# The second MLP product of a decoder layer with the tokens stationary and 512 weight columns moving

## The chip, the core and the metric

The kernel runs on one core of a Trainium2 chip. The core has a matrix engine (TensorE; PE in the profile, and PEld for its weight loads), a vector engine (VectorE, DVE), a scalar engine (ScalarE, ACT), GpSimd (POOL, hardly used here) and a sync engine (SyncE, SP) that issues nearly all memory transfers (DMA). A matmul holds one operand, of up to 128 columns, still in TensorE's array (stationary, brought in by a weight load) and streams the columns of the other through it (moving); the result goes to PSUM, whose banks hold 512 fp32 values per partition. The other engines work in SBUF, which has 128 partitions. The metric is the device time of one execution in microseconds (us); here and below "median" is that of the repeated runs.

## The reference

One hybrid decoder layer and a final norm, in float32, for 256 tokens of width 2048. The part that matters here is the MLP and the last norm:

```python
h2 = _modulate(_rms_norm(x, norm2_g[l]), shift2, scale2)
ff = jnp.square(jax.nn.relu(jnp.einsum("bsd,df->bsf", h2, w_ff1[l])))
x = x + gate2[:, None, :] * jnp.einsum("bsf,fd->bsd", ff, w_ff2[l])
return _rms_norm(x, final_g)
```

`w_ff1` is 2048 x 8192, `w_ff2` 8192 x 2048. The six vectors shift1 to gate2 come from `silu(c) @ w_ada + b_ada`. Ahead of this stand a norm, a wide input projection, a linear recurrence, sliding-window attention and an output projection, which are the same in both kernels.

## The kernel before, in words

The activations lie with the channels on the partitions: a tile `x1[f]` holds 128 channels of the 256 tokens (sixteen of them). Weights are stationary, 128 x 128 at a time, and 256 tokens move. To keep float32 accuracy at a cheaper product, each operand is split into a rounded part and the exact rest (`float32r`), and each product is made of three passes: rounded x rounded, rounded x rest, rest x rounded (lines L176, L177, L178, in `gemm`).

From the projection on, the work is a stream of *units*. A unit is 1 MB of weights, 128 partitions x 2048 columns: it is loaded into one of four `raw` (rw) buffers (L152), split in two halves of 1024 columns, the rounded part by ScalarE (L160, wh) and the rest by VectorE (L162, wl), into three buffers each, and multiplied on TensorE, 48 matmuls of 256 columns. Weights are taken in two units ahead. Side work of the other engines is spread over the units from a list (`later`), and so is the making of the conditioning vector (`ada_unit`, 1 MB of `w_ada` and one VectorE reduction at L241). A scheduler sets the final order of each engine's queue from the data dependencies and the buffers; an engine then works its queue in order.

The MLP runs in four quarters `c`. A quarter makes 16 tiles of the hidden layer (`ff1_unit`, matmuls L656 to L658; evicted by L660 to L664 and split by L141, L142 into `ff[c, f]`), and then adds their share of the second product into all 16 tiles of x1 (`ff2_unit`). A second-product unit makes one output tile: its weights are stationary, the 16 hidden tiles move, and VectorE evicts with the gate and the sum in one operation:

```python
ps = gemm(w, 0, [ff[c, j] for j in range(16)])
ve.scalar_tensor_tensor(out=x1[f], in0=ps, scalar=mod[:, 5 * KT + f:5 * KT + f + 1], in1=x1[f],
                        op0=ALU.mult, op1=ALU.add)
```

In the first quarter each such unit first forces the conditioning unit of its own gate (`flush(5 * KT + f + 1)`). In the last quarter ScalarE squares each finished tile and VectorE sums the squares (L134, L135); ScalarE then multiplies the tile with the norm's g (L684).

At the end the squares are summed over the partitions by matmuls with a column of ones (L754), and the 16 tiles are turned to token rows by 32 transposes on TensorE (L747), because 1/rms is then a scalar per partition: `rstd_cols` (L104 to L110) makes it, VectorE and ScalarE scale eight tiles of 128 tokens x 512 channels out of PSUM (L762, L764), and SP stores them (L765).

## Time and profile before

| | |
|---|---|
| median of 3 runs | 1605.51 us (1603.79 to 1606.83) |
| span of the profiled execution | 1604.2 us |
| granted TensorE clock, mean | 0.992 |
| TensorE, matmuls | 1567.8 us busy, 98% |
| VectorE / ScalarE | 73% / 53% busy |
| memory traffic | 388.27 MB, mean 242 GB/s |

The profile is of one execution, whose own time is its span, 1604.2 us, from the first to the last instruction; it is 1.3 us under the median. In rows of instructions stand the start, the length (both us), the engine, the line, the operation, the output and inputs with their shapes, and in brackets the idle time ahead of it with what ended it. Groups give the count, the mean length in ns, and the idle time before. In the tables by stage stand, after the stretch and its length, busy time and count of PE, PEld, DVE, ACT and POOL, then the granted clock as a share, the DMA engines' share, and GB/s. Matmuls are pipelined: one that is listed with 0.28 us can start 0.12 us after the one ahead. The pitch from start to start is what counts.

### The profile page before, as it was taken

The page shows a single profiled execution, that of the slowest core. Times are in us where ns is not written, and L with a number is a line of the kernel's source. Part 1 is how long each engine was busy: PE and PEld are TensorE (multiplying, and loading weights), DVE is VectorE, ACT ScalarE, POOL GpSimd, SP SyncE. Part 2 cuts the span into 40 slices and gives each one's busy share as a digit, 9 for nine tenths or more (in the row PEclk, how much of TensorE's full clock was granted, in tenths as well). Part 3 has the DMA queues.
Part 4 walks back from the last instruction along what each step waited for, and adds up shares of the span by engine and source line. Part 5 has one row for each costly group of instructions (what it writes and reads, how often), then busy time and mean ns, then how long its engine had stood idle before and what let it go on. Part 6 is the DMA issues. An engine that isn't in the chain of part 4 may idle for free.

```text
span 1604.2 us, 30912 instructions
## 1 busy us (share of the span) xinstructions
PE 1567.8 (98%) x12924; PEld 1542.5 (96%) x12924; DVE 1168.7 (73%) x1830; ACT 849.0 (53%) x1345; POOL 0.2 (0%) x4
## 2 busy tenths in 40 slices
PE   5999999999999999999999999999999999999998
PEld 4999998899999999999999999999999999999998
DVE  7798998898989678688787666865555555555554
ACT  5733447786886463344455553355434553355554
POOL 0000000000000000000000000000000000000000
PEclk7999999999999999999999999999999999999999
DMA  8898976557777777777976666865555555555552
GB/s 323 337 341 317 339 263 213 196 190 232 288 257 264 283 261 292 276 286 278 335 290 242 237 237 245 345 224 184 184 184 185 184 184 185 184 184 184 184 184 79
DMA packets 61724, 388.27 MB, mean 242 GB/s; under 512 B 6576, under 2 KB 11024, under 8 KB 19216
## 3 DMA queue, kind: packets, MB, share of 16 engines
q1 hardware_dynamic: 57168, 381.95, 65.6%
q10 hardware_dynamic: 4416, 4.35, 0.9%
q8 instruction: 101, 1.65, 0.4%
q14 instruction: 39, 0.32, 0.1%
HBM read 384.13 MB, written 2.15 MB: 241 GB/s over the span
## 4 chain that ended last, share of the span: by engine, by line
PE 86%; DVE 6%; DMA 3%; ACT 2%; issue 2%; SPq 0%; ACTq 0%; DVEq 0%
PE pg L178 20%; PE pg L176 20%; PE pg L177 20%; PE pg L656 8%; PE pg L657 8%; PE pg L658 8%; DMA ra<-in_wada_dram 2%; DVE wl L162 2%; PE pg L186 1%; DVE ra L241 1%; ACT wh L160 1%; PE pa L470 1%; PE pa L477 1%; DVE k L536 1%; DMA rw<-in_w_p_dram 0%
## 5 line engine op out<-in xcount | busy, mean ns | idle before, releaser
L160 ACT ACTIVATE wh<-rw 128x1024 fp32r<-128x1024 f32 (+2 forms) x534 | 545.5, 1023 | 656.4 <-PE pg L177 446.9
L176 PE MATMUL pg<-k,wh 128*128 128x256 f32 x3072 | 867.3, 283 | 11.0 <-ACT k L141 9.0
L178 PE MATMUL pg<-k,wl 128*128 128x256 f32 x3072 | 862.9, 282 | 3.5 <-DVE wl L162 3.3
L177 PE MATMUL pg<-k,wh 128*128 128x256 f32 x3072 | 865.0, 282 | 0.3 <-DVE k L142 0.2
L162 DVE TENSOR_TENSOR wl<-rw,wh 128x1024 fp32r<-128x1024 f32 (+2 forms) x534 | 628.4, 1178 | 286.7 <-ACT wh L160 285.0
L176 PEld LDWEIGHTS pg<-k,wh 128*128 128x128 f32 x3072 | 580.1, 189 | 13.8 <-ACT k L141 9.5
L178 PEld LDWEIGHTS pg<-k,wl 128*128 128x128 f32 x3072 | 580.3, 189 | 6.2 <-DVE wl L162 4.9
L177 PEld LDWEIGHTS pg<-k,wh 128*128 128x128 f32 x3072 | 580.2, 189 | 1.6 <-DVE k L142 0.9
L656 PE MATMUL pg<-z,wh 128*128 128x258 f32 x1024 | 289.8, 283 | 0.0
L657 PE MATMUL pg<-z,wh 128*128 128x256 f32 x1024 | 289.1, 282 | 0.0
L658 PE MATMUL pg<-z,wl 128*128 128x258 f32 x1024 | 288.5, 282 | 0.0
L241 DVE CUSTOM_DVE_ANT_0 ra<-ra,scr,vc 128x2048 f32<-128x2048 f32 x96 | 225.0, 2346 | 16.0 <-DMA ra<-in_wada_dram 15.9
L658 PEld LDWEIGHTS pg<-z,wl 128*128 128x128 f32 x1024 | 194.9, 190 | 0.0
L657 PEld LDWEIGHTS pg<-z,wh 128*128 128x128 f32 x1024 | 194.4, 190 | 0.0
L656 PEld LDWEIGHTS pg<-z,wh 128*128 128x128 f32 x1024 | 193.7, 189 | 0.0
L673 DVE SCALAR_TENSOR_TENSOR k<-pg,mod,k 128x256 f32<-128x256 f32 x64 | 30.9, 483 | 38.9 <-PE pg L178 38.9
L660 DVE TENSOR_REDUCE sh<-pg 128x1 f32<-128x2 f32 x64 | 10.2, 159 | 37.6 <-PE pg L658 37.6
L663 ACT ACTIVATE t<-t,sh 128x256 f32<-128x256 f32 x64 | 31.7, 496 | 1.4 <-DVE t L662 1.4
L142 DVE TENSOR_TENSOR k<-t,k 128x256 fp32r<-128x256 f32 x64 | 27.2, 425 | 4.7
L314 DVE TENSOR_TENSOR k<-pg,k 128x256 f32<-128x256 f32 x64 | 25.8, 418 | 6.6 <-PE pg L178 4.0
L141 ACT ACTIVATE k<-k 128x256 fp32r<-128x256 f32 x64 | 24.3, 411 | 9.7 <-DVE k L602 5.6
L186 PE MATMUL pg<-k,rw 128*128 128x256 f32 x128 | 28.3, 379 | 0.0
(146 smaller groups left out, 755.5 us busy)
## 6 DMA issues: line engine op xcount, KB each, us to landing
rw<-in_w_f_dram SPq DMA_DIRECT2D x204, 1024.0 KB, 4.8
ra<-in_wada_dram SPq DMA_DIRECT2D x96, 1024.0 KB, 6.2
rw<-in_w_p_dram SPq DMA_DIRECT2D x31, 1024.0 KB, 5.7
rw<-in_w_r_dram SPq DMA_DIRECT2D x20, 768.0 KB, 4.6
rw<-in_w_r_dram SPq DMA_DIRECT2D x16, 640.0 KB, 4.3
bt<-ud ACTq DMA_DIRECT2D x8, 512.0 KB, 4.5
xt<-in_xt_dram SPq DMA_DIRECT2D x8, 256.0 KB, 5.4
lw<-in_lruw_dram SPq DMA_DIRECT2D x4, 512.0 KB, 6.3
```

Source lines behind the costliest of these rows:

```text
L160: se.activation(wh[:, :c], raw[:, o:o + c], AF.Copy)
L162: ve.tensor_tensor(out=wl[:, :c], in0=raw[:, o:o + c], in1=wh[:, :c].bitcast(F32), op=ALU.subtract)
L176: te.matmul(ps, lhsT=wh[:, w], rhs=hl[:, 0], start=k == 0, stop=False)
L177: te.matmul(ps, lhsT=wh[:, w], rhs=hl[:, 1], start=False, stop=False)
L178: te.matmul(ps, lhsT=wl[:, w], rhs=hl[:, 0], start=False, stop=k == n - 1)
L186: te.matmul(ps, lhsT=raw[:, e:e + P], rhs=xs[k // 2][:, k % 2], start=k == k0, stop=k == k1 - 1)
L241: r = ve.tensor_tensor_reduce(out=raw, in0=raw, in1=scr, scale=1.0, scalar=vc[:, V_BADA + c:V_BADA + c + 1], op0=ALU.mult, op1=ALU.add, ac ...
L656: te.matmul(ps, lhsT=wh[:, e], rhs=z[k][:, 0:258], start=k == 0, stop=False)
L657: te.matmul(ps[:, 0:256], lhsT=wh[:, e], rhs=z[k][:, 258:514], start=False, stop=False)
L658: te.matmul(ps, lhsT=wl[:, e], rhs=z[k][:, 0:258], start=False, stop=k == KT - 1)
L663: se.activation(t[:, 0], t[:, 0], AF.Relu, bias=sh)
L673: ve.scalar_tensor_tensor(out=x1[f], in0=ps, scalar=mod[:, 5 * KT + f:5 * KT + f + 1], in1=x1[f], op0=ALU.mult, op1=ALU.add)
```

## The change

The second product is turned round. The hidden layer's tokens become stationary (128 hidden channels x 128 tokens) and 512 weight columns move, so the output has tokens on the partitions and 512 channels in a full PSUM bank. A unit is still 1 MB, but now the weights of four output tiles x four hidden tiles; they are read from the same array in memory as four runs of 512 columns per partition. Its two halves of 1024 weights each hold two hidden tiles for all 512 output columns, and a matmul moves four runs of 128 columns. Four units `u` finish one block `q` of 512 output channels for the two token blocks `b`, which lie in two PSUM banks. The sums over the quarters stand in eight tiles `acc`: copied there by ScalarE in the first quarter, added by VectorE after. x1 is turned to token rows (`turn_x1`, tiles `xk`) beside the first quarter. Since gate2 and the last norm's g now run along the free dimension, they are made as lines that are the same on every partition, by a product of ones with a diagonal (`gate2_line`, `line_of`), beside the last quarter; there the gate, the residual sum, the square with its sum, and g are applied to each block. At the end only 1/rms remains, and eight scalings and stores.

The diff, without comments that were removed and without the loop that tells the two kinds of loads apart:

```diff
+    def w_load_rows(src):
+        raw = wp.tile([P, 4, 512], F32, tag="raw", name=nm("rw"), bufs=RAW_BUFS)
+        nc.sync.dma_start(out=raw, in_=src)
+        parts = []
+        for o in (0, 256):
+            wh = wp.tile([P, 4, 256], F32R, tag="wh", name=nm("wh"), bufs=WH_BUFS)
+            se.activation(wh, raw[:, :, o:o + 256], AF.Copy)
+            wl = wp.tile([P, 4, 256], F32R, tag="wl", name=nm("wl"), bufs=WH_BUFS)
+            ve.tensor_tensor(out=wl, in0=raw[:, :, o:o + 256], in1=wh.bitcast(F32), op=ALU.subtract)
+            parts.append((wh, wl))
+        return parts
...
+    def add_rows(run, q, u):
+        f0 = full[0] + 4 * q
+        units.append((run, w_f[f0:f0 + 4, :, u * 512:u * 512 + 512].rearrange("f p n -> p f n"), 2048, None))
+        if q == 3 and u == 3:
+            full[0] += 16
...
-    def ff2_unit(c, f):
+    xk, acc, g2b, gfb, cur2 = {}, {}, {}, {}, {}
+    ssf = sp.tile([P, 2, 4], F32, tag="ssf", name="ssf", bufs=1)
+
+    def turn_x1(q):
+        for b in range(2):
+            pt = bank([P, 512])
+            for i in range(4):
+                te.transpose(pt[:, i * P:(i + 1) * P], x1[4 * q + i][:, b * P:(b + 1) * P], idt)
+            xk[b, q] = kp.tile([P, 512], F32, tag="k2", name=nm("xk"))
+            se.activation(xk[b, q], pt, AF.Copy)
+
+    def gate2_line(q):
+        g2b[q] = line_of(mod[:, 5 * KT + 4 * q:5 * KT + 4 * q + 4])
+        gfb[q] = line_of(vc[:, V_GF + 4 * q:V_GF + 4 * q + 4])
+
+    def line_of(cols):
+        pc = bank([P, 512])
+        dg = tmp([P, 512])
+        ve.tensor_tensor(out=dg.rearrange("p (k f) -> p k f", k=4), in0=idt[:, None, :].broadcast_to((P, 4, P)),
+                         in1=cols[:, :, None].broadcast_to((P, 4, P)), op=ALU.mult)
+        te.matmul(pc, lhsT=ones, rhs=dg, start=True, stop=True)
+        o = kp.tile([P, 512], F32, tag="k2", name=nm("ln"))
+        se.activation(o, pc, AF.Copy)
+        return o
+
+    def ff2_unit(c, q, u):
         def run(w):
+            if c == 3 and u == 0:
+                if q == 0:
+                    flush(6 * KT)
+                later(1.0, gate2_line, q)
+            if u == 0:
+                for b in range(2):
+                    cur2[b] = pg.tile([P, 512], F32, tag="pg", name=nm("pg"))
+            for k in range(4):
+                wh, wl = w[k // 2]
+                e = slice(k % 2 * P, k % 2 * P + P)
+                hl = ff[c, 4 * u + k]
+                first, last = u == 0 and k == 0, u == 3 and k == 3
+                for b in range(2):
+                    t = slice(b * P, b * P + P)
+                    te.matmul(cur2[b], lhsT=hl[:, 0, t], rhs=wh[:, :, e], start=first, stop=False)
+                    te.matmul(cur2[b], lhsT=hl[:, 0, t], rhs=wl[:, :, e], start=False, stop=False)
+                    te.matmul(cur2[b], lhsT=hl[:, 1, t], rhs=wh[:, :, e], start=False, stop=last)
+            if u < 3:
+                return
+            for b in range(2):
+                if c == 0:
+                    acc[b, q] = kp.tile([P, 512], F32, tag="k2", name=nm("ac"))
+                    se.activation(acc[b, q], cur2[b], AF.Copy)
+                else:
+                    ve.tensor_tensor(out=acc[b, q], in0=cur2[b], in1=acc[b, q], op=ALU.add)
+                if c == 3:
+                    o, x_ = acc[b, q], xk[b, q]
+                    ve.tensor_tensor(out=o, in0=o, in1=g2b[q], op=ALU.mult)
+                    ve.tensor_tensor(out=o, in0=o, in1=x_, op=ALU.add)
+                    se.activation(x_, o, AF.Square, accum_out=ssf[:, b, q:q + 1])
+                    ve.tensor_tensor(out=o, in0=o, in1=gfb[q], op=ALU.mult)
             if c == 0:
-                flush(5 * KT + f + 1)
-            ps = gemm(w, 0, [ff[c, j] for j in range(16)])
...
-        add_unit(run)
+                later(1.0, turn_x1, q)
+        add_rows(run, q, u)
...
-    def turn(n):
...
-    rs3 = rstd_cols(pq)
+    ss3 = sp.tile([P, 2], F32, tag="ss1", name="ss3", bufs=1)
+    ve.tensor_reduce(out=ss3, in_=ssf, axis=mybir.AxisListType.X, op=ALU.add)
+    rs3 = rstd_cols(ss3)
     for n in range(8):
         q, b = divmod(n, 2)
-        pt = turned[n] if n < 2 else turn(n)
...
+        o = acc[b, q]
+        if n % 2:
+            se.activation(o, o, AF.Copy, scale=rs3[:, b:b + 1])
+        else:
+            ve.tensor_scalar(out=o, in0=o, scalar1=rs3[:, b:b + 1], scalar2=None, op0=ALU.mult)
         nc.sync.dma_start(out=out[b, :, q * 512:(q + 1) * 512], in_=o)
```

Up to the first second-product matmul the queues of all engines hold the same instructions in the same order. Three places differ in what the prediction speaks of. In the changed kernel the three passes of the second product are L733, L734 and L735, the transposes of x1 L697, the lines' diagonals and products L709 and L711, the sum over the quarters L743, the gate L746, the residual L747, the square L748, g L749, and the last sum, scalings and stores L815, L821 and L823, L824.

TensorE, the start of the second product in the first quarter, before (k is a hidden tile, pg the PSUM tile of the output):

```order
L177 MATMUL pg_11382<-k_10334,wh_11238 128x256
L178 MATMUL pg_11382<-k_10334,wl_11240 128x256
L176 MATMUL pg_11382<-k_10405,wh_11238 128x256
L177 MATMUL pg_11382<-k_10405,wh_11238 128x256
L178 MATMUL pg_11382<-k_10405,wl_11240 128x256
```

and in the changed kernel:

```order
L734 MATMUL pg_11383<-wl_11241,k_10335 128x512
L735 MATMUL pg_11383<-wh_11239,k_10335 128x512
L733 MATMUL pg_11384<-wh_11239,k_10335 128x512
L734 MATMUL pg_11384<-wl_11241,k_10335 128x512
L735 MATMUL pg_11384<-wh_11239,k_10335 128x512
L733 MATMUL pg_11383<-wh_11239,k_10406 128x512
```

One hidden tile now serves two groups of three matmuls, one for each block of tokens, and each matmul is twice as wide.

VectorE, between the first and the second product of the last quarter, before (wl is a rest part of weights; the first row is the last eviction of the first product):

```order
L662 TENSOR_TENSOR t_17542<-pg_17491,rs_10267 128x256
L162 TENSOR_TENSOR wl_17485<-rw_17481,wh_17483 128x1024
L142 TENSOR_TENSOR k_17546<-t_17542,k_17546 128x256
L162 TENSOR_TENSOR wl_17489<-rw_17481,wh_17487 128x1024
L673 SCALAR_TENSOR_TENSOR k_9190<-pg_17559,mod,k_9190 128x256
```

and in the changed kernel (L709's outputs t are the diagonals; the second product's splits are L178):

```order
L682 TENSOR_TENSOR t_16407<-pg_16356,rs_10268 128x256
L709 TENSOR_TENSOR t_16451<-idt,mod 128x512
L178 TENSOR_TENSOR wl_16350<-rw_16346,wh_16348 128x1024
L142 TENSOR_TENSOR k_16411<-t_16407,k_16411 128x256
L709 TENSOR_TENSOR t_16457<-idt,vc 128x512
L709 TENSOR_TENSOR t_16611<-idt,mod 128x512
L178 TENSOR_TENSOR wl_16354<-rw_16346,wh_16352 128x1024
L709 TENSOR_TENSOR t_16617<-idt,vc 128x512
L709 TENSOR_TENSOR t_16771<-idt,mod 128x512
L709 TENSOR_TENSOR t_16777<-idt,vc 128x512
L178 TENSOR_TENSOR wl_16418<-rw_16414,wh_16416 128x1024
L709 TENSOR_TENSOR t_16931<-idt,mod 128x512
```

All eight diagonals stand here, among the splits of the second product's first units; before, only the splits and the first eviction stood there. TensorE's two products with them follow the first unit of each block.

VectorE, the end of the program, before (from the last eviction on):

```order
L673 SCALAR_TENSOR_TENSOR k_10173<-pg_18498,mod,k_10173 128x256
L104 TENSOR_SCALAR st_18566<-pa_18561 128x2
L106 RECIPROCAL st_18566<-st_18566 128x2
L108 SCALAR_TENSOR_TENSOR st_18566<-st_18566 128x2
L109 TENSOR_TENSOR st_18566<-st_18566 128x2
```

and in the changed kernel:

```order
L743 TENSOR_TENSOR ac_11994<-pg_16904,ac_11994 128x512
L743 TENSOR_TENSOR ac_11996<-pg_16905,ac_11996 128x512
L746 TENSOR_TENSOR ac_11994<-ac_11994,ln_16934 128x512
L746 TENSOR_TENSOR ac_11996<-ac_11996,ln_16934 128x512
L747 TENSOR_TENSOR ac_11994<-ac_11994,xk_12003 128x512
L747 TENSOR_TENSOR ac_11996<-ac_11996,xk_12010 128x512
L749 TENSOR_TENSOR ac_11994<-ac_11994,ln_16940 128x512
L749 TENSOR_TENSOR ac_11996<-ac_11996,ln_16940 128x512
L815 TENSOR_REDUCE ss_17034<-ssf 128x2
L104 TENSOR_SCALAR st_17036<-ss_17034 128x2
```

Nine operations now stand between the last product and the first step to 1/rms, where one stood (its square and the matmuls with ones, on the other engines, stood there too).

More of the change, by code (lines that the diff above doesn't have):

```diff
@@ L666, in ff1_unit @@
         add_unit(run)
-    def ff2_unit(c, f):
-        def run(w):
-            if c == 0:
-                flush(5 * KT + f + 1)
-            ps = gemm(w, 0, [ff[c, j] for j in range(16)])
-            ve.scalar_tensor_tensor(out=x1[f], in0=ps, scalar=mod[:, 5 * KT + f:5 * KT + f + 1], in1=x1[f],
-                                    op0=ALU.mult, op1=ALU.add)
-            if c == 3:
-                if f == 0:
-                    stat[3] = sp.tile([P, T], F32, tag="asq", name=nm("asq"), bufs=1)
-                if f < 15:
-                    sumsq(stat[3], x1[f], f == 0)
-                else:
-                    stat[4] = tmp([P, T])
-                    se.activation(stat[4], x1[f], AF.Square)
-                se.activation(x1[f], x1[f], AF.Copy, scale=vc[:, V_GF + f:V_GF + f + 1])
-        add_unit(run)
+    xk, acc, g2b, gfb, cur2 = {}, {}, {}, {}, {}
@@ L713, in hybrid_layer @@
             ff1_unit(c, f)
-        for f in range(16):
-            ff2_unit(c, f)
+        for q in range(4):
+            for u in range(4):
+                ff2_unit(c, q, u)
     ready, credit, ada_credit = {}, 0.0, 0.0
@@ L720, in hybrid_layer @@
             if j not in ready:
-                ready[j] = w_dma(*units[j][1:3])[0] if units[j][3] else w_load(*units[j][1:3])
+                if units[j][3] is None:
+                    ready[j] = w_load_rows(units[j][1])
+                else:
+                    ready[j] = w_dma(*units[j][1:3])[0] if units[j][3] else w_load(*units[j][1:3])
         if n == n_ya:
@@ L740, in hybrid_layer @@
             ada_credit -= 1
-    def turn(n):
-        q, b = divmod(n, 2)
-        pt = bank([P, 512]) if n % 2 else pg.tile([P, 512], F32, tag="pg", name=nm("pt"))
-        for i in range(4):
-            te.transpose(pt[:, i * P:(i + 1) * P], x1[4 * q + i][:, b * P:(b + 1) * P], idt)
-        return pt
-    turned = [turn(n) for n in range(2)]
-    pq = bank([P, 2])
-    for b in range(2):
-        for n in (3, 4):
-            te.matmul(pq[:, b:b + 1], lhsT=stat[n][:, b * P:(b + 1) * P], rhs=ones[:, 0:1], start=n == 3, stop=n == 4)
-    rs3 = rstd_cols(pq)
+    ss3 = sp.tile([P, 2], F32, tag="ss1", name="ss3", bufs=1)
+    ve.tensor_reduce(out=ss3, in_=ssf, axis=mybir.AxisListType.X, op=ALU.add)
+    rs3 = rstd_cols(ss3)
     for n in range(8):
         q, b = divmod(n, 2)
-        pt = turned[n] if n < 2 else turn(n)
-        o = tmp([P, 512])
-        ca = 256 if n == 0 else 512 if n % 2 else 0
-        if ca > 0:
-            se.activation(o[:, :ca], pt[:, :ca], AF.Copy, scale=rs3[:, b:b + 1])
-        if ca < 512:
-            ve.tensor_scalar(out=o[:, ca:], in0=pt[:, ca:], scalar1=rs3[:, b:b + 1], scalar2=None, op0=ALU.mult)
+        o = acc[b, q]
+        if n % 2:
+            se.activation(o, o, AF.Copy, scale=rs3[:, b:b + 1])
+        else:
+            ve.tensor_scalar(out=o, in0=o, scalar1=rs3[:, b:b + 1], scalar2=None, op0=ALU.mult)
         nc.sync.dma_start(out=out[b, :, q * 512:(q + 1) * 512], in_=o)
```

## The prediction

> **What bounds the kernel now.** I read the page first (busy shares, clock), then the table by stages, then the timeline of TensorE inside the second product, and last the chain of waits at the end.
>
> ```profile
> PE 1567.8 (98%) x12924; PEld 1542.5 (96%) x12924; DVE 1168.7 (73%) x1830; ACT 849.0 (53%) x1345; POOL 0.2 (0%) x4
> PEclk7999999999999999999999999999999999999999
> 965.00:1060.00 95.00, 95.00 (x803) 95.00 (x803) 71.00 (x74) 37.45 (x39) 0.00 (x0) 1.00 0.79 298
> 1330.00:1420.00 90.00, 90.00 (x760) 90.00 (x759) 46.85 (x50) 34.65 (x35) 0.00 (x0) 1.00 0.54 188
> 1510.00:1604.20 94.20, 86.64 (x736) 86.35 (x734) 48.40 (x65) 43.94 (x63) 0.00 (x0) 0.98 0.39 138
> ```
>
> TensorE is busy for 98% of the span at full clock. The last three rows are stretches of the second product, in the first, third and last quarter of the MLP (columns: length, then busy time and count on PE, PEld, DVE, ACT, POOL, then clock, DMA share, GB/s). In the third quarter PE has no gap, DVE works 47 us of 90, ACT 35, and the DMA engines are 0.54 busy; in the first quarter, with more loads, PE has none either. So this stage is set by TensorE's own pitch, and only what changes that pitch, or starves it, can move the time. The pitch:
>
> ```profile
> 1560.96 0.28 PE L177 MATMUL pg<-k,wh 128*128 128x256 f32 x1
> 1560.96 0.19 PEld L178 LDWEIGHTS pg<-k,wl 128*128 128x128 f32 x1
> 1561.08 0.28 PE L178 MATMUL pg<-k,wl 128*128 128x256 f32 x1
> 1561.08 0.19 PEld L176 LDWEIGHTS pg<-k,wh 128*128 128x128 f32 x1
> 1561.19 0.28 PE L176 MATMUL pg<-k,wh 128*128 128x256 f32 x1
> ...
> 1507.15 0.48 DVE L673 SCALAR_TENSOR_TENSOR k<-pg,mod,k 128x256 f32<-128x256 f32 x1 [0.64 <-PE pg L178]
> ...
> 1592.26 0.48 DVE L673 SCALAR_TENSOR_TENSOR k<-pg,mod,k 128x256 f32<-128x256 f32 x1 [4.29 <-PE pg L178]
> ```
>
> Each matmul has its own weight load, and a load starts as the matmul ahead of it starts, so it runs under that one. Sixteen evictions of the last quarter stand from 1507.15 to 1592.26: 85.11/15 = 5.674 us for one unit of 48 matmuls, 118.2 ns each. Is it the 256 columns that take 118.2 ns, or the load of 128 weights? These rows decide:
>
> ```profile
> 1592.22 0.44 PE pt L747 x4
> 1593.38 0.70 PE pa L754 x6
> 101.12 6.91 PE pg L186 x32
> 7.51 0.19 PEld L203 LDWEIGHTS pa<-t,ones 128*128 128x128 f32 x1 [0.24 <-issue]
> 7.94 0.19 PEld L203 LDWEIGHTS pa<-t,ones 128*128 128x128 f32 x1 [0.24 <-issue]
> 8.37 0.19 PEld L203 LDWEIGHTS pa<-t,ones 128*128 128x128 f32 x1 [0.24 <-issue]
> ```
>
> They are pieces of the chain of waits and loads of the first microseconds. L754 moves ONE column per matmul and still takes 0.70/6 = 117 ns; L747 moves 128 and takes 110. So 110 to 118 ns is the price of loading 128 weights, whatever moves. L186 are the four-pass products, each issued as two instructions that stream 256 columns twice: 6.91/32 = 215.9 ns for 512 column steps, each with a weight load of the usual length. L203 does the same with 512 columns: 430 ns for 1024 steps. The 512 steps more take 214 ns, 0.418 each, and L186 has 2 ns beside its steps; 256 steps need 107 ns. So the second product now waits for its weight loads.
>
> **The change, part by part.** *The products.* (L697 and above are lines of the changed kernel where they are said to be new; all others are the kernel before's.) Before: 64 units x 5.674 = 363.1 us. After: 64 units of 24 matmuls, 1536 in all, each with one load of 128 stationary columns and 512 moving ones. The load (118 at most) goes under a stream of 512 steps. I take L186's 215.9 ns, since it is 512 steps with a load for each: 331.7 us, 31.4 us less. Bounds: 214 ns, were L186's small rest to vanish (3 us less); 225, if the 118.2 were 107 plus 11 that every matmul pays (14 us more); 236, twice 118.2, if column steps set it now (nothing gained). The moving operand is four runs of 128 columns, which no row shows; those ends cover that too.
>
> The Trainium skill's "TensorE: Matmul & The Clock Gate", section "Back-to-back issue gap", gives N/2.4 + 2.5 ns for an isolated matmul: 216 at 512 columns, as L186 has it, but 109 at 256, where this trace has 118.2. The same section gives about 131 ns for a sustained stream of 512 columns; by it the products would take 201 us. L203's 430 ns for twice 512 speaks against that (a rival, below).
>
> *The two lines.* Eight new products of ones with a 512-column diagonal (L711), in the last quarter. They are L203's form, two instructions of 430 ns: 8 x 0.86 = 6.9 us on a TensorE that has no idle time. Their operands come from eight VectorE operations that stand just after the last first-product eviction, each L201's 0.68 us, 5.5 us together:
>
> ```profile
> L201 DVE TENSOR_TENSOR t<-idt,sc x4: 682/684/691, 3.5 to 5.3; 128x512 f32<-128x512 f32 x4
> L160 ACT ACTIVATE wh<-rw x534: 402/1060/1080, 22.5 to 1583.6; 128x1024 fp32r<-128x1024 f32 x166, 128x512 fp32r<-128x512 f32 x7, 128x256 fp32r<-128x256 f32 x5
> L162 DVE TENSOR_TENSOR wl<-rw,wh x534: 396/1224/1228, 23.6 to 1584.7; 128x1024 fp32r<-128x1024 f32 x166, 128x512 fp32r<-128x512 f32 x7, 128x256 fp32r<-128x256 f32 x5
> ```
>
> Behind them wait the splits of the next weights. A half unit is 2.59 us of products; with three buffers a half freed now is wanted two halves, 5.18 us, later and needs 1.06 (ACT) + 1.22 (DVE) = 2.3 us, so 2.9 us may stand ahead of a split before TensorE waits. The eight go in groups of one to three between splits, at most 2.05 us: hidden, with about 1 us to spare. Without that cover it is a few microseconds, once. The four evictions' operations of 0.68 us go two or three at a time and are hidden alike. In the last quarter's four units DVE has 8 x 1.22 + 8 x 0.68 = 15.2 us of work in 20.7.
>
> *The 32 transposes of x1* move from the end into the first quarter: 32 x 0.11 = 3.5 us, on TensorE's path there. What they leave at the end is counted next.
>
> *The tail.* Before, from the start of the last product to the finished 1/rms:
>
> ```profile
> 1591.93 0.28 PE L178 MATMUL pg<-k,wl 128*128 128x256 f32 x1
> 1592.26 0.48 DVE L673 SCALAR_TENSOR_TENSOR k<-pg,mod,k 128x256 f32<-128x256 f32 x1 [4.29 <-PE pg L178]
> 1594.11 0.16 DVE L104 TENSOR_SCALAR st<-pa 128x2 f32<-128x2 f32 x1 [1.37 <-PE pa L754]
> 1595.13 0.16 DVE L110 SCALAR_TENSOR_TENSOR st<-st 128x2 f32<-128x2 f32 x1
> 1596.46 4.47 SPq L765 DMA_DIRECT2D out_dram<-t  x8
> L216 ACT ACTIVATE t<-xt x4: 627/629/634, 9.4 to 12.9; 128x512 f32<-128x512 f32 x4
> L216 ACT ACTIVATION_READ_ACCUMULATOR t<-xt x4: 186/193/206, 9.9 to 13.4; 128x1 f32 x4
> L222 DVE TENSOR_SCALAR xt<-xt,st x8: 481/481/489, 15.0 to 17.8; 128x512 f32<-128x512 f32 x8
> ```
>
> 3.4 us (1591.93 to 1595.29). After: block 0's last matmul starts 3 x 0.216 = 0.65 us ahead of block 1's last (time zero). The first add (L743) can start 0.44 after its matmul (0.33 as before, and 0.11 for the longer stream), at -0.2. Six operations of 0.68 bring both blocks to x + gated sum at 3.9; block 1's square with its accumulator read takes 0.82 on ACT to 4.8, while DVE does the two products with g and is done at about 5.5 (the last one waits for its square). Reduce 0.16, then L104 to L110's 1.2 as before: 6.9. That is 3.5 us more. From there on it stays: the first scaling takes 0.48 (L222's) where a half tile took as much, and the eight stores are bound by their issue, 4.47 us for 8, not by the scalings.
>
> *The weight loads from memory.* Each is still 1 MB, but in 512 pieces of 2 KB in place of 128 of 8 KB, and 1.049 MB each 5.18 us is 202 GB/s. The nearest rows with 2 KB pieces are those of the load of the tokens, 512 of 2048 columns at a time:
>
> ```profile
> L95 SPq DMA_DIRECT2D xt<-in_xt_dram x8: 424/432/665, 1.6 to 5.2; - x8
> 3.00:5.00 2.00, 0.73 (x1) 0.50 (x2) 1.65 (x4) 1.70 (x3) 0.00 (x0) 1.00 0.82 224
> 5.00:6.00 1.00, 1.00 (x2) 0.34 (x1) 1.00 (x2) 0.00 (x0) 0.00 (x0) 1.00 0.81 223
> rw<-in_w_f_dram SPq DMA_DIRECT2D x204, 1024.0 KB, 4.8
> ```
>
> 224 GB/s with the DMA engines 0.82 busy, so 224 to 273. At 273 a load takes 3.8 us of 5.18, and the loads are issued units ahead, so their 4.8 us to landing doesn't show. I cost this at nothing; VectorE's split covers it, for it is what a late load would hold, and TensorE after it. If the cover went, TensorE would stand for what a load takes over 5.18 (a rival, below). The conditioning units of gate2, 1 MB each, stood one beside each unit in the first quarter (298 GB/s, share 0.79 above, PE still full); now there are about 0.3 per unit, into the second quarter. An 8 KB-piece load costs the engines 1.049/(188/0.54) = 3.0 us, so the first quarter needs (3.8 + 0.3 x 3.0)/5.18 = 0.91 of them: tight, but with buffers several units deep ahead of it.
>
> The sum: -31.4 + 6.9 + 3.5 + 3.5 = -17.5 us. The profiled execution's span is 1604.2, 1.3 us under the median of the runs shown, 1605.51. So 1586.7 in the profile's terms and **1588.0 us** as a median.
>
> **The rivals.** *Every matmul pays 11 ns beside its columns* (8%). Then 225 ns: 345.6 us, 17.5 less, minus the 13.9 added: -3.6, 1601.9. For it, the first product's units, whose matmuls are the same but for two more columns in two of three:
>
> ```profile
> 1049.03 0.16 DVE L660 TENSOR_REDUCE sh<-pg 128x1 f32<-128x2 f32 x1 [0.29 <-PE pg L658]
> 1054.79 0.16 DVE L660 TENSOR_REDUCE sh<-pg 128x1 f32<-128x2 f32 x1 [0.68 <-PE pg L658]
> ```
>
> 5.76 us for 48 is 120.0 ns, so columns do show a little. Against it: L186's 2 ns.
>
> *The columns set the pitch already* (5%), the four runs of 128 included: 236 ns, products 363.1 as before, and the 13.9 us added remain: 1619.4, slower. Above 349.2/1536 = 227 ns the change loses. For it: no matmul here reads its moving operand in four runs. Against: L754's one column at 117.
>
> *The weights come late* (9%). Pieces of 2 KB lie 1 MB apart from one to the next, where the tokens' rows lie 8 KB apart. If a load gets no more than the 184 to 188 GB/s that the stage moves now, a unit takes 1.049/184 = 5.70 us: 364.8 + 13.9 - 363.1 = +15.6, 1621, slower. It decides from 192 GB/s down (349.2/64 = 5.46 us). Against: 224 at a share of 0.82. The Trainium skill's "DMA: Bandwidth & Descriptors", section "Latency and other measured facts", speaks for this rival: rows at a pitch of 512 KB read at 207 of 214 GB/s, at 2 MB at 164. No run here shows such a pitch; by its ratios the 273 would fall to some 210 to 264, an estimate, still over 202.
>
> *The load stays the pitch* (1%): 512 columns pass in the time of a weight load, 118.2 ns. Then 1536 x 0.1182 = 181.6, and 363.1 - 181.6 - 13.9 = 167.6 us less, 1437.9. For it only that 256 columns do so now; against it L186 and L203. The Trainium skill's section on the issue gap, named above, is near this case with its 131 ns.
>
> *The change is partly eaten by waits* (5%): half of the 31 us lost to splits and line products that come late, 1604.
>
> **How the numbers follow.** The forecast has 72%; its own range is 1582 (214 ns, the 1.7 us by which the fastest run shown lies under the median, and 1 us of tail counted too much) to 1593 (5 us of waits). With the first rival and the one of waits, 1582 to 1604 holds 8 in 10; the slower cases lie beyond. About 0.2% (3.2 us) can be told from no change. The changes within 0.2% come from the first rival, whose 1601.9 is at that edge, and the waits. Faster: 72 + 1 + 4 (half of the first rival) + 3 = 80; same: 4 + 2 = 6; slower: 14, the two rivals at 1619 and 1621.
>
> **What would show it.** In the changed profile the second product's matmuls should start 216 ns apart, with weight loads that leave PEld well under PE in those stretches, and a unit take 5.18 us. L711's products should take 0.86 us each and L697's transposes 0.11. PE should still show no idle time there; DMA should stand near 200 GB/s at a share of 0.75. From the last product to L110's end it should be 6.9 us. A pitch over 227, waits of the split for a load of rw, or a granted clock under 1.00 in those stretches would prove me wrong.

## The result, and the profile after

The changed kernel takes 1611.12 us (median of 5 runs, 1609.95 to 1612.14) against 1605.51 for the kernel before: ratio 1.0036, 95% interval 1.0025 to 1.0047. It is slower by about 0.4%, where 1.1% faster was forecast. The span of the profiled execution, the longest of the five, is 1610.3 us, 6.1 above the 1604.2 of before. Its time is 1612.14 us, 1.8 above its span, so the span of before, 1604.2, was not that execution's time either; the forecast, 17.5 us under the median, does not depend on it.

From the page of the changed kernel:

```profile
PE 1566.4 (97%) x11396; PEld 1469.2 (91%) x11396; DVE 1167.0 (72%) x1809; ACT 852.3 (53%) x1352; POOL 0.2 (0%) x4
PEclk7999999999999999999999999999999999999998
```

And its table by stages, stretches of the second product in the first, second, third and last quarter (the second and the third end some 8 us inside the next quarter's first product, the last holds the end of the program):

```profile
950.00:1045.00 95.00, 95.00 (x439) 77.92 (x438) 53.15 (x47) 43.37 (x50) 0.00 (x0) 1.00 0.68 235
1140.00:1235.00 95.00, 95.00 (x447) 78.73 (x446) 49.81 (x48) 37.29 (x37) 0.00 (x0) 1.00 0.59 200
1325.00:1415.00 90.00, 90.00 (x420) 74.47 (x419) 45.14 (x43) 34.90 (x35) 0.00 (x0) 1.00 0.57 190
1510.00:1610.00 100.00, 85.50 (x360) 67.21 (x358) 54.91 (x69) 39.17 (x54) 0.00 (x0) 0.94 0.37 126
```

TensorE stays busy without a gap up to the last product, at full clock, and the DMA engines are less than 0.7 busy. Nothing comes late. The weight loads do leave PEld below PE now (74 of 90 us), as they should. The loss is in TensorE's own pitch. The timeline in the third quarter:

```profile
1344.91 0.39 PE L733 MATMUL pg<-wh,k 128*128 128x512 f32 x1
1344.91 0.19 PEld L734 LDWEIGHTS pg<-wl,k 128*128 128x128 f32 x1
1345.14 0.39 PE L734 MATMUL pg<-wl,k 128*128 128x512 f32 x1
1345.14 0.19 PEld L735 LDWEIGHTS pg<-wh,k 128*128 128x128 f32 x1
1345.37 0.40 PE L735 MATMUL pg<-wh,k 128*128 128x512 f32 x1
...
1340.37 1.28 DVE L743 TENSOR_TENSOR ac<-pg,ac 128x512 f32<-128x512 f32 x2
1362.61 1.28 DVE L743 TENSOR_TENSOR ac<-pg,ac 128x512 f32<-128x512 f32 x2
1384.85 1.28 DVE L743 TENSOR_TENSOR ac<-pg,ac 128x512 f32<-128x512 f32 x2
```

The loads still run under the matmul ahead, but the matmuls start 0.23 us apart. The sums of two neighbouring blocks stand 22.24 us apart, which is 96 matmuls: **231.7 ns each**, not 215.9. Four units (one block) take 22.24 us, one unit 5.56. The 64 units take 64 x 5.56 = 355.8 us in place of 363.1: the turn gains 7.3 us, not 31.4.

The parts that the change adds came nearly as forecast. In the first quarter a block has eight transposes beside it, in the last one two lines:

```profile
974.42 0.60 ACT L741 ACTIVATE ac<-pg 128x512 f32<-128x512 f32 x1 [1.04 <-PE pg L735]
997.56 0.60 ACT L741 ACTIVATE ac<-pg 128x512 f32<-128x512 f32 x1 [1.04 <-PE pg L735]
...
1523.20 1.28 DVE L743 TENSOR_TENSOR ac<-pg,ac 128x512 f32<-128x512 f32 x2
1547.14 1.28 DVE L743 TENSOR_TENSOR ac<-pg,ac 128x512 f32<-128x512 f32 x2
```

A block takes 23.14 us in the first quarter, 0.90 more, so 4 x 0.90 = 3.6 us for 32 transposes; and 23.94 in the last, 1.70 more, so 6.8 us for the lines. The tail, from the start of the last product to the finished 1/rms:

```profile
1595.10 0.40 PE L735 MATMUL pg<-wh,k 128*128 128x512 f32 x1
...
1594.84 1.39 DVE L743 TENSOR_TENSOR ac<-pg,ac 128x512 f32<-128x512 f32 x2 [5.27 <-PE pg L735]
1596.15 1.28 DVE L746 TENSOR_TENSOR ac<-ac,ln 128x512 f32<-128x512 f32 x2
1597.35 1.28 DVE L747 TENSOR_TENSOR ac<-ac,xk 128x512 f32<-128x512 f32 x2
1598.82 1.30 DVE L749 TENSOR_TENSOR ac<-ac,ln 128x512 f32<-128x512 f32 x2 [0.19 <-ACT xk L748]
1601.26 0.16 DVE L110 SCALAR_TENSOR_TENSOR st<-st 128x2 f32<-128x2 f32 x1
```

1595.10 to 1601.42 is 6.3 us where 3.4 stood before: 3.0 more (6.32 - 3.36, and 6.9 was forecast). Together: -7.3 + 3.6 + 6.8 + 3.0 = +6.1 us, and 1604.2 + 6.1 = 1610.3, the span. That close a fit is partly luck, since the spans of the five executions run from 1608.2 to 1610.3, but no large part is missing. What has to be found out is why a matmul of 512 columns takes 231.7 ns.

### The profile page after: what moved, and what is told of

It is laid out like the page before. It is cut to its first block, busy times and chain, and to the rows that moved or that the text cites. A ratio compares the mean times of both kernels' runs of the same rounds, so it can differ in the third digit from the quotient of the medians.

```text
span 1610.3 us, 27801 instructions
## 1 busy us (share of the span) xinstructions
PE 1566.4 (97%) x11396; PEld 1469.2 (91%) x11396; DVE 1167.0 (72%) x1809; ACT 852.3 (53%) x1352; POOL 0.2 (0%) x4
## 4 chain that ended last, share of the span: by engine, by line
PE 89%; DVE 5%; DMA 2%; ACT 2%; issue 1%; SPq 0%; ACTq 0%; DVEq 0%
PE pg L191 13%; PE pg L189 13%; PE pg L190 13%; PE pg L676 8%; PE pg L677 8%; PE pg L678 8%; PE pg L733 7%; PE pg L734 7%; PE pg L735 7%; PE pg L199 2%; DVE wl L162 2%; DMA ra<-in_wada_dram 1%; PE pa L490 1%; PE pa L497 1%; DVE ra L254 1%
## 5 line engine op out<-in xcount | busy, mean ns | idle before, releaser
L160 ACT ACTIVATE wh<-rw 128x1024 fp32r<-128x1024 f32 (+2 forms) x406 | 409.6, 1012 | 453.8 <-PE pg L190 240.2
L162 DVE TENSOR_TENSOR wl<-rw,wh 128x1024 fp32r<-128x1024 f32 (+2 forms) x406 | 472.0, 1164 | 175.2 <-ACT wh L160 173.1
L189 PE MATMUL pg<-k,wh 128*128 128x256 f32 x2048 | 580.1, 284 | 11.1 <-ACT k L141 9.0
L191 PE MATMUL pg<-k,wl 128*128 128x256 f32 x2048 | 576.2, 282 | 4.3 <-DVE wl L162 4.3
L190 PE MATMUL pg<-k,wh 128*128 128x256 f32 x2048 | 577.2, 282 | 0.7 <-DVE k L142 0.7
L189 PEld LDWEIGHTS pg<-k,wh 128*128 128x128 f32 x2048 | 386.8, 189 | 13.8 <-ACT k L141 9.5
L191 PEld LDWEIGHTS pg<-k,wl 128*128 128x128 f32 x2048 | 387.4, 190 | 7.1 <-DVE wl L162 5.7
L190 PEld LDWEIGHTS pg<-k,wh 128*128 128x128 f32 x2048 | 387.5, 189 | 1.9 <-DVE k L142 1.2
L178 DVE TENSOR_TENSOR wl<-rw,wh 128x1024 fp32r<-128x1024 f32 x128 | 156.7, 1225 | 154.2 <-ACT wh L176 154.2
L176 ACT ACTIVATE wh<-rw 128x1024 fp32r<-128x1024 f32 x128 | 135.8, 1061 | 203.9 <-PE pg L735 181.7
L733 PE MATMUL pg<-wh,k 128*128 128x512 f32 x512 | 203.9, 398 | 0.0
L734 PE MATMUL pg<-wl,k 128*128 128x512 f32 x512 | 201.9, 394 | 0.0
L735 PE MATMUL pg<-wh,k 128*128 128x512 f32 x512 | 201.3, 393 | 0.0
L733 PEld LDWEIGHTS pg<-wh,k 128*128 128x128 f32 x512 | 96.2, 188 | 23.0 <-issue 0.7
L734 PEld LDWEIGHTS pg<-wl,k 128*128 128x128 f32 x512 | 96.3, 188 | 22.5 <-issue 1.0
```

The source lines that it names most:

```text
L160: se.activation(wh[:, :c], raw[:, o:o + c], AF.Copy)
L162: ve.tensor_tensor(out=wl[:, :c], in0=raw[:, o:o + c], in1=wh[:, :c].bitcast(F32), op=ALU.subtract)
L189: te.matmul(ps, lhsT=wh[:, w], rhs=hl[:, 0], start=k == 0, stop=False)
L190: te.matmul(ps, lhsT=wh[:, w], rhs=hl[:, 1], start=False, stop=False)
L191: te.matmul(ps, lhsT=wl[:, w], rhs=hl[:, 0], start=False, stop=k == n - 1)
L733: te.matmul(cur2[b], lhsT=hl[:, 0, t], rhs=wh[:, :, e], start=first, stop=False)
```

## The experiments

**Theories.** The prediction took its price from L186, a plain float32 product. The second product's operands are float32r. So: (A) the moving operand in four runs of 128 columns costs the 16 ns; (S) float32r columns themselves stream at about 0.45 ns each, so that columns, not weight loads, already set the 118.2 ns before; (B) the weight load beside the stream, or other traffic in SBUF, slows it; (L) the prediction's own, that the load of 128 weights is what set the 118.2.

### One run of 512 columns

The weights are laid out in memory so that a unit is one block with rows of 8 KB and a matmul moves 512 neighbouring columns.

```diff
-                e = slice(k % 2 * P, k % 2 * P + P)
+                e = slice(k % 2 * 512, k % 2 * 512 + 512)
...
-                    te.matmul(cur2[b], lhsT=hl[:, 0, t], rhs=wh[:, :, e], start=first, stop=False)
+                    te.matmul(cur2[b], lhsT=hl[:, 0, t], rhs=wh[:, e], start=first, stop=False)
```

> The changed kernel with the weights of each second-product unit laid out in memory so that a unit is one block of 128 rows of 8 KB, and a matmul moves one run of 512 columns instead of four runs of 128. All else is as in the change. Theory A (the four runs of 128 columns cost the 16 ns a matmul that came over 215.9): the evictions of one block of the third quarter stand 20.7 us apart instead of 22.24, 1536 x 16 ns = 24 us less, about 1587 us. Theory B (the stream of float32r columns, or the weight load beside it, costs it whatever the runs): 22.2 us, a time within 2 us of the changed kernel's 1611. Theory C (the memory's 2 KB pieces cost something that no wait shows): the time falls, but the matmul's pitch stays at 231.7 ns. I expect A as likely as B.

1609.83 us, ratio to the kernel before 1.0037 (1.0023 to 1.0051). Two evictions of the third quarter, and then the loads of the MLP's weights in the view of the DMA issues (count, size, median us to landing):

```profile
1337.53 1.28 DVE L740 TENSOR_TENSOR ac<-pg,ac 128x512 f32<-128x512 f32 x2
1359.77 1.28 DVE L740 TENSOR_TENSOR ac<-pg,ac 128x512 f32<-128x512 f32 x2
```

```profile
rw<-in_w_f_dram SPq DMA_DIRECT2D x204, 1024.0 KB, 4.9
```

22.24 us as in the change: theory A is out. With pieces of 8 KB the loads land in 4.9 us, and with pieces of 2 KB in the change in 5.1; the ratio to the kernel before is 1.0037 here and 1.0036 there, so C is out too.

### Half a weight load

```diff
-                    t = slice(b * P, b * P + P)
+                    m = 64 if c == 2 else P
+                    t = slice(b * P, b * P + m)
+                    o = cur2[b][0:m]
...
```

The other 64 rows of that quarter's share are left out of the sums, so this kernel serves for its times alone.

> In the third quarter of the MLP the stationary operand of the second product is 64 tokens instead of 128, so a weight load brings half the columns and the moving stream of 512 stays; rows 64 to 127 of that quarter's share are left out of the sums. Theory B1 (the weight load beside the stream disturbs it): the pitch in the third quarter falls from 231.7 to about 224 (half of the 16 ns), the other quarters stay at 231.7. Theory B2 (the float32r columns take 0.443 ns each themselves) and theory A (the four runs): 231.7 in all quarters.

Two evictions of the third quarter, each of 64 rows:

```profile
1337.48 1.27 DVE L746 TENSOR_TENSOR ac<-pg,ac 64x512 f32<-64x512 f32 x2
1359.64 1.27 DVE L746 TENSOR_TENSOR ac<-pg,ac 64x512 f32<-64x512 f32 x2
```

22.16 us: 230.8 ns. Half the load takes 1 ns off, not 8. That speaks for B2 (the columns themselves), but is not nothing; a run below carries it on.

### bfloat16 parts in one quarter

```diff
-            ff[c, f] = split(t[:, 1])
+            ff[c, f] = split(t[:, 1], dt=BF16 if c == 2 else F32R)
...
+        units.append((run, w_f[...], 2048, BF16 if c == 2 else F32R))
```

> In the third quarter of the MLP both operands of the second product are bfloat16 tiles instead of float32r ones, of the same shapes and runs (the parts are rounded to bfloat16, so the rests are less exact there); a column is then 2 bytes per partition, and a weight load half the bytes. Theory A (four runs of 128 columns): still about 231.7 ns in that quarter. Theory B (4-byte columns, by the stream or by the load beside it): about 216. The other quarters stay at 231.7.

The third quarter, evictions and a piece of the timeline:

```profile
1337.45 1.28 DVE L746 TENSOR_TENSOR ac<-pg,ac 128x512 f32<-128x512 f32 x2
1358.17 1.28 DVE L746 TENSOR_TENSOR ac<-pg,ac 128x512 f32<-128x512 f32 x2
...
1350.13 0.38 PE L737 MATMUL pg<-wl,k 128*128 128x512 bf16 x1
1350.13 0.10 PEld L738 LDWEIGHTS <-k 128*128 128x128 bf16 x1
1350.34 0.38 PE L738 MATMUL pg<-wh,k 128*128 128x512 bf16 x1
```

20.72 us a block, 215.8 ns a matmul: the price that the prediction took. Same shapes, same runs, same order; only the type differs. The time of that one run, 1604.37 us, is 6.8 below the change's median; one quarter's share is 384 x 15.9 ns = 6.1.

The Trainium skill's "TensorE: Matmul & The Clock Gate", section "Back-to-back issue gap", has N/2.4 + 2.5 ns for an isolated matmul, 216 at 512 columns. The bfloat16 stream agrees, and the float32r stream, at 231.7, does not. The 131 ns that the section gives for a sustained stream is not reached by either, though each matmul here follows the one ahead without a gap.

### Columns cut to pieces

Each second-product matmul, but for the first and last of a sum, is cut by columns, another way in each block.

```diff
+WIDTHS = [[(0, 4)], [(0, 2), (2, 4)], [(0, 3), (3, 4)], [(0, 1), (1, 2), (2, 3), (3, 4)]]
...
+                    for pas, (st, mv) in enumerate(((0, wh), (0, wl), (1, wh))):
+                        f_, l_ = first and pas == 0, last and pas == 2
+                        for f0, f1 in [(0, 4)] if f_ or l_ else WIDTHS[q]:
+                            te.matmul(cur2[b][:, f0 * P:f1 * P], lhsT=hl[:, st, t], rhs=mv[:, f0:f1, e],
+                                      start=f_, stop=l_)
```

> Every second-product matmul but the first and last of a sum is cut by columns: block 0 of each quarter moves 512 at once as in the change, block 1 256 and 256, block 2 384 and 128, block 3 four times 128; each piece has its own weight load, and the sums are the same. The pitch per width is read from the trace. Theory B2 (columns at 0.443 ns and 4.8 ns a matmul): 118.2 at 256, 175 at 384, and for 128 the load's floor, 110 or above. Theory D (0.417 ns a column, with a floor of some 110 to 118 from the load, and an extra stall that only long streams have): 109 to 118 at 256, 160 to 165 at 384. Theory A: one run more or less costs 5 ns, so 256 in two runs is 112, 384 in three is 172.

The one execution took 2397.11 us, and no price can be read from it, for its granted clock was low from the start, long before the cut part:

```profile
0.00:400.00 400.00, 380.87 (x2070) 345.46 (x2070) 262.10 (x513) 154.14 (x314) 0.20 (x4) 0.62 0.61 221
1200.00:1700.00 500.00, 500.00 (x2738) 474.49 (x2737) 201.76 (x235) 164.15 (x217) 0.00 (x0) 0.63 0.43 150
```

The clock column reads 0.62 and 0.63 where it is 1.00 in the changed kernel. It was low for some 1300 us before the first cut matmul, so the cut can't have begun it within this execution; what did can't be told from one run. The same cut in the third quarter alone (`if f_ or l_ or c != 2`):

> The cut by columns again, in the third quarter of the MLP alone (block 0 whole, block 1 twice 256, block 2 384 and 128, block 3 four times 128 columns), each piece with its own weight load of 128 columns; the rest is the change. Theory L, the prediction's (a weight load costs 110 to 118 ns and is the floor of a matmul): four pieces of 128 take 4 x 110 to 118 = 440 to 472 ns, the 256s 118.2. Theory S (the load hides, and every float32r column costs about 0.45 ns): 128 columns take 55 to 60 ns, 256 118, 384 174, 512 231.7, so the four blocks of that quarter take about the same time, 22.2 us each and 0.5 at most more.

The mean clock was 0.991, and the blocks can be read:

```profile
1339.07 1.28 DVE L748 TENSOR_TENSOR ac<-pg,ac 128x512 f32<-128x512 f32 x2
1361.69 1.28 DVE L748 TENSOR_TENSOR ac<-pg,ac 128x512 f32<-128x512 f32 x2
1388.80 1.50 DVE L748 TENSOR_TENSOR ac<-pg,ac 128x512 f32<-128x512 f32 x2 [0.26 <-PE pg L739]
1430.50 0.69 DVE L748 TENSOR_TENSOR ac<-pg,ac 128x512 f32<-128x512 f32 x1 [1.54 <-PE pg L739]
```

The blocks end at these rows: the second took 22.62 us, the third 27.11, the fourth 41.70. Of 96 products in a block 92 are cut, and the four whole ones take 0.93. So twice 256 columns take (22.62 - 0.93)/92 = 235.8 ns, 117.9 each; four times 128 take (41.70 - 0.93)/92 = 443.2, **110.8 each**; and 384 with 128 take 284.6. If the 128 cost 110.8 there too, the 384 cost 173.8, which is 0.4526 ns a column, the same as 231.7/512 = 0.4525.

Where the loads stand tells the two limits apart. Rows from the second and the fourth block, each a run of loads and then the matmuls that they are for:

```profile
1345.47 0.54 PEld L739 LDWEIGHTS pg<-wh,k 128*128 128x128 f32 x4
1345.59 0.63 PE L739 MATMUL pg<-wh,k 128*128 128x256 f32 x4
...
1395.12 0.97 PEld L739 LDWEIGHTS pg<-wh,k 128*128 128x128 f32 x8
1395.18 1.06 PE L739 MATMUL pg<-wh,k 128*128 128x128 f32 x8
```

With 256 columns a load is listed 0.12 us ahead of its matmul, one whole matmul: it starts as the one ahead starts (3 ns after, the median of 161 loads; the same 3 ns stand at 512 columns and in the kernel before). With 128 columns it starts 52 ns after the one ahead (the median of 322), a little less than 128 columns take by the price above. That is how it would look if a matmul were listed from the end of the stream ahead of it and then stood for its weights, at 128 columns and not at 256. So read, the block of 384 and 128 fits too: its matmuls are listed 227 and 60 ns apart in turn, but its loads 178 and 108, near the 173.8 and 110.8 above. This is a reading of the listing; no run tests it by itself.

Both theories are half right. Matmuls of 128 columns with a float32r load of 128 each come no closer than 110.8 ns, as L said, and S's 55 to 60 ns is wrong. But this floor lies below the 118 ns of 256 columns. The widths tried fit one rule: a matmul takes whichever is longer, its load or its columns; before the change that was the columns, by 7 ns.

### TensorE alone

Twelve units in a row use weights that are already split.

```diff
+                if 0 < j - q0 <= 12:
+                    ready[j] = [ready[q0][1]] * 2
+                    continue
...
```

These units' sums are of the wrong weights, and the kernel serves for its times alone.

> In the third quarter units 1 to 12 of the second product use the split weights of unit 0's second half again, so that for some 60 us no weights are loaded from memory and none are split: TensorE works with ScalarE, VectorE and the DMA engines nearly at rest (those units' sums are then of the wrong weights). Theory S1 (the float32r stream is slowed by other engines' and the DMA's use of SBUF): 216 ns in that stretch. Theory S2 (the stream's own rate): 231 to 232 ns as in the other quarters.

The middle of the third quarter in the table by stages, and then two evictions:

```profile
1345.00:1385.00 40.00, 40.00 (x175) 32.43 (x174) 2.77 (x4) 0.00 (x0) 0.00 (x0) 1.00 0.00 0
```

```profile
1338.39 1.38 DVE L743 TENSOR_TENSOR ac<-pg,ac 128x512 f32<-128x512 f32 x2 [16.45 <-PE pg L735]
1360.63 1.39 DVE L743 TENSOR_TENSOR ac<-pg,ac 128x512 f32<-128x512 f32 x2 [20.86 <-PE pg L735]
```

For 40 us VectorE works 2.8 us, ScalarE and the DMA engines not at all, and the block still takes 22.24 us. Other work in SBUF has no part in it.

### Loads of 128, 64, 32 and 8 columns

```diff
+                    m = (128, 64, 32, 8)[q] if c == 2 else P
+                    t = slice(b * P, b * P + m)
+                    o = cur2[b][0:m]
...
```

The rows that are not loaded are left out of that quarter's sums.

> In the third quarter the stationary operand has 128, 64, 32 and 8 tokens in blocks 0 to 3 (the other rows of that quarter's share are left out), so that a weight load brings as many columns; the moving 512 float32r columns stay. Half a load had taken 1.0 ns off (230.7). Theory S2a (the moving stream's own rate): about 230 to 232 ns at every size. Theory S2b (part of the 16 ns comes from the load that runs beside the stream): the pitch falls steadily with the load, to 216 to 222 at 8 columns.

```profile
1339.42 1.28 DVE L746 TENSOR_TENSOR ac<-pg,ac 128x512 f32<-128x512 f32 x2
1361.58 1.27 DVE L746 TENSOR_TENSOR ac<-pg,ac 64x512 f32<-64x512 f32 x2
1383.74 1.27 DVE L746 TENSOR_TENSOR ac<-pg,ac 32x512 f32<-32x512 f32 x2
1405.86 1.27 DVE L746 TENSOR_TENSOR ac<-pg,ac 8x512 f32<-8x512 f32 x2
```

The evictions (of 128, 64, 32 and 8 rows) are 22.16, 22.16 and 22.12 us apart: 230.8, 230.8 and 230.4 ns. A load of a sixteenth leaves the pitch where half a load had put it. So S2a: the float32r stream has this rate whatever is loaded beside it, and the load accounts for 1.3 ns of the 16 at most. The moving and the held operand changed type together, so which of the two types sets the rate is not shown.

### bfloat16 parts in both kernels

The whole second product with bfloat16 parts, turned (as the change) and not (as the kernel before). This is less exact, and serves to compare the two forms without the float32r rate.

> The change with both operands of the whole second product as bfloat16 parts instead of float32r parts (rounded part and rounded rest, three passes as before; less exact). From the third quarter's 215.9 ns in the run before: 1536 x (231.7 - 215.9) = 24.3 us less than the change, 1611.1 - 24.3 = 1586.8 us.

> The kernel before, its second product likewise with bfloat16 parts: stationary weights, 256 moving token columns. Theory L (the weight load of 128 columns sets the pitch): a load of half the bytes may be shorter, but by the prediction the one-column matmul's 110 to 118 ns remains, so 118.2 ns stays and the time is that of before, 1605. Theory S (columns set the pitch): 256 columns at the 0.4216 ns that 512 bfloat16 columns took are 107.9 ns, 109 with a little beside them; 3072 x 9.2 to 10.3 = 28 to 32 us less, 1574 to 1577 us, and the turned product is then the slower one by 10 to 12 us in bfloat16 too.

On the same chip the turned form takes 1586.99 us, ratio to the kernel before 0.9871 (0.9855 to 0.9887), and the plain one 1579.00, ratio 0.9817 (0.9797 to 0.9837). From the plain one's third quarter:

```profile
1313.47 0.48 DVE L676 SCALAR_TENSOR_TENSOR k<-pg,mod,k 128x256 f32<-128x256 f32 x1 [0.42 <-PE pg L181]
...
1392.07 0.48 DVE L676 SCALAR_TENSOR_TENSOR k<-pg,mod,k 128x256 f32<-128x256 f32 x1 [0.42 <-PE pg L181]
```

Sixteen evictions in 78.60 us: 5.24 us a unit, 109.2 ns a matmul. 3072 x 9.0 = 27.7 us less. The change of type alone, without the turn, brings nearly the 31.4 us that were forecast from the turned products, and with this type the turned form is 8 us slower than the plain one (by the parts 9.4: 13.4 added, and 1536 x 215.8 against 3072 x 109.2, 4.0 gained). (Here the loads are shorter too, 0.10 us listed against 0.19, so this run alone would not tell load from columns at 256; the cut columns do.)

### The added work taken off again

First the lines by the memory, in place of the diagonals and products:

```diff
+        nc.scalar.dma_start(out=ld.rearrange("f p -> p f"), in_=ml)
...
-        te.matmul(pc, lhsT=ones, rhs=dg, start=True, stop=True)
...
+        nc.scalar.dma_start(out=o, in_=ld[4 * i:4 * i + 4].rearrange("f p -> (f p)")[None, :].broadcast_to((P, 512)))
```

> The change, with the lines of gate2 and of the norm's g made by the memory instead of TensorE: the 32 columns are stored to a scratch array in memory at the end of the third quarter, and eight transfers read them back to all partitions; the eight products of ones with a diagonal and their eight VectorE operations are gone. If the sum of the parts holds, the four pairs of 1.70 us leave TensorE's path: 6.8 us less than the change, 1611.1 - 6.8 = 1604.3 us. If the products stood where TensorE would have waited anyway, less than 2 us.

1604.05 us, ratio 0.9990 (0.998 to 1.000). The last quarter's first two evictions:

```profile
1523.84 1.28 DVE L747 TENSOR_TENSOR ac<-pg,ac 128x512 f32<-128x512 f32 x2
1546.07 1.28 DVE L747 TENSOR_TENSOR ac<-pg,ac 128x512 f32<-128x512 f32 x2
```

22.23 us a block in place of 23.94: the 1.70 us are gone, four times.

Then the tail as well (of its diff the order in the last unit, the operations moved ahead, and those that stay behind the last product):

```diff
+            if (c, q, u) == (3, 3, 3):
+                kb = [(k, b) for b in range(2) for k in range(4)]
...
+            if c == 3 and u == 2:
+                for b in range(2):
+                    ve.tensor_tensor(out=acc[b, q], in0=acc[b, q], in1=g2b[q], op=ALU.mult)
+                    ve.tensor_tensor(out=acc[b, q], in0=acc[b, q], in1=xk[b, q], op=ALU.add)
...
+                    ve.tensor_tensor(out=x_, in0=cur2[b], in1=g2b[q], op=ALU.mult)
+                    ve.tensor_tensor(out=o, in0=o, in1=x_, op=ALU.add)
...
+        if q == 3:
+            ve.scalar_tensor_tensor(out=o, in0=o, scalar=rs3[:, b:b + 1], in1=gfb[q], op0=ALU.mult, op1=ALU.mult)
```

> The kernel of the run before, and the tail shortened: the sum over three quarters is multiplied by the gate and added to x1 before the last unit of a block, so two operations instead of three stand behind the last product; the last unit finishes block 0 of the tokens before block 1; and the last block's g goes into its final scaling. The tail from the last product's start to the finished 1/rms, 6.3 us in the change and 3.4 before, should be 4.0: 0.44 to the first operation, 2 x 0.68, the square 0.82, the sum 0.16, 1.2 for 1/rms. Then 1604.3 - 2.3 = 1602.0 us, 3.5 us under the kernel before: the turned product's 7.3 us less the transposes' 3.5 and 0.6 of tail.

1601.99 us (median of 11 runs), ratio 0.9979, interval 0.9970 to 0.9987. Its tail:

```profile
1587.15 0.40 PE L742 MATMUL pg<-wh,k 128*128 128x512 f32 x1
...
1587.58 0.69 DVE L757 TENSOR_TENSOR xk<-pg,ln 128x512 f32<-128x512 f32 x1 [1.37 <-PE pg L742]
1588.31 0.69 DVE L758 TENSOR_TENSOR ac<-ac,xk 128x512 f32<-128x512 f32 x1
1591.01 0.16 DVE L110 SCALAR_TENSOR_TENSOR st<-st 128x2 f32<-128x2 f32 x1
```

1587.15 to 1591.17: 4.0 us. This version beats both kernels with float32r parts, by 0.2% of the kernel before; that is all that the 7.3 us of gain leave once the rest is trimmed. With bfloat16 parts:

> The same with both operands of the second product as bfloat16 parts (less exact). From 1587.0 us of the change in bfloat16: 1587.0 - 6.8 - 2.3 = 1577.9 us, against 1579.0 of the kernel before in bfloat16: the turned form then gains nothing over the plain one, because 256 bfloat16 columns already take 109.2 ns and 512 take 215.9, 2.5 ns less than twice that: 3.9 us in all, and the transposes and the tail cost 4.1.

1577.91 us, ratio 0.9825 (0.9812 to 0.9839); the plain form's ratio was 0.9817 (0.9797 to 0.9837), in another comparison with the kernel before. The two can't be told apart: trimmed, the turned form is no better than the plain one.

## Why the prediction was wrong, point by point

- *TensorE's own pitch sets the stage, without gaps, at full clock.* Right, before and after.
- *"So the second product now waits for its weight loads."* This step failed. The rows under it, one column at 117 ns and 128 at 110, do show a floor: with float32r loads it measures 110.8 ns. But the 118.2 ns stand 7 above it, and they are 256 float32r columns at 0.46 ns: the product waited for its columns. The prediction treated "110 to 118" as one price, and so took a small gap between two limits for no gap. Part of the gap was hidden by a reading: 0.70/6 = 117 divides the length of a merged row, which holds the 0.25 us for which the last matmul is listed, by its count. From start to start the one-column matmuls at 1593.38 and after stand 112 ns apart in the same trace, and the transposes 109, so the rows gave 109 to 112 for a float32 load and left 6 to 9 ns of the 118.2 unexplained. A hint was quoted under the first rival: 120.0 ns in the first product, for a mean of 1.3 columns more; a pitch set by the load would not move with columns. It is a hint only, for 1.3 columns at 0.45 ns are 0.6 of these 1.8 ns.
- *"I take L186's 215.9 ns, since it is 512 steps with a load for each."* This is the term of the sum that was mis-sized: 231.7 ns, 355.8 us in place of 331.7, a loss of 24.1 us against the forecast. 215.9 is right for plain float32 steps and, as it turned out, for bfloat16 columns; float32r columns were never priced from a row with float32r in it. The only rows that had it were the 118.2 and the 120.0.
- *The bounds*, 214 to 236, held 231.7, but the upper one was there for "column steps set it now", which the prediction argued against. But the range of the time stopped at 1604, because "the columns set the pitch already" had 5%.
- *The four runs of 128 columns*: cost nothing (one run: the same 22.24 us).
- *The lines*: 6.9 forecast, 6.8 measured, and 1604.05 us once they left TensorE. Their diagonals on VectorE were hidden, as said.
- *The transposes*: 3.5 forecast, 3.6 measured.
- *The tail*: 3.5 more forecast, 3.0 measured.
- *The weight loads in 2 KB pieces cost nothing*: right. The stage moves 190 GB/s at a share of 0.57 where 0.75 was forecast; 190/0.57 = 333 GB/s at full share, not the 273 that the rows at the program's start gave.
- *The rivals.* "The columns set the pitch already" named the mechanism and the side; its 236 ns (twice 118.2) and 1619.4 us were too high, because two matmuls of 256 cost 4.7 ns more than one of 512. "Every matmul pays 11 ns beside its columns" is refuted: what float32r takes over bfloat16 grows with the columns, from 9.0 ns at 256 to 15.9 at 512. "The weights come late", "the load stays the pitch" and waits: none is in the trace.

With 231.7 in place of 215.9 the prediction's own sum gives 1604.2 - 7.3 + 13.9 = 1610.8, against 1610.3: the other terms were right to within 0.5 us each, and two of them, the lines and the tail, were tested by taking them off again.

## What to carry to other kernels

Price a matmul from rows of the same operand type as well as the same shape: here 512 columns took 215.8 ns in bfloat16 and 231.7 in float32r, and that alone turned a gain of 1% into a loss. Where two limits lie within a few per cent of each other (110.8 for the load, 118.2 for the columns), it has to be known which of them sets the pitch before one of them is taken away: look for rows in which only one of them changes, read from start to start, and for whether a load starts with the matmul ahead of it or later. Work that is put on the engine that bounds the kernel (lines, transposes, a longer tail) could be costed to within 0.5 us from like rows here; it needs a gain that is as sure.

## What the runs showed of the hardware that was not expected

- A moving float32r column takes 0.4525 ns at full clock where a bfloat16 one takes 0.4216 (231.7 and 215.8 ns for 512), with other engines at rest, in one run or four, and beside a load of 8 columns (230.4). The portions are uneven: eight in ten float32r matmuls start 227 to 236 ns apart, also with the other engines at rest, where the bfloat16 ones keep to 215 and 216. Why is open. It may be its four bytes; against bytes alone, the four-pass float32 product keeps 0.42 ns a step, but there two steps share a column. No run here gave the two operands different types.
- With a weight load of 128 float32r columns each, matmuls of 128 columns take 110.8 ns; listed, a load is 0.19 us in float32r and 0.10 in bfloat16, so the floor of bfloat16 loads may lie lower, but was not measured; it is at most the 109.2 that 256 bfloat16 columns took.
- One execution of a kernel whose second product had many more loads had a granted clock of 0.63 throughout and took 2397 us. The same cut in one quarter did not. What brought it about is open.
